# A float32 decoder layer on one core: FFN down products in three parts instead of two, three of eight row pairs by Strassen's seven products

## The chip, the cores and the metric

The kernel runs on one core of one Trainium2 chip. The metric is device time in microseconds (us). Engines are named as in the profile: PE is TensorE (matrix products), PEld its weight loads, DVE VectorE, ACT ScalarE, POOL GpSimd, SP the engine that issues nearly all transfers.

## The reference

One layer on 256 tokens of width 2048, all float32: a half-step FFN, a mixer (attention beside a convolution), a second FFN. Only the FFNs matter here:

```python
def swiglu_ffn(x, w_gate, w_up, w_down):      # 2048 -> 5632 -> 2048
    h = jax.nn.silu(x @ w_gate) * (x @ w_up)
    return h @ w_down

x = layer_norm(ALPHA * x + 0.5 * swiglu_ffn(x, ...), ln1_g, ln1_b)
...
x = layer_norm(ALPHA * x + 0.5 * swiglu_ffn(x, ...), ln3_g, ln3_b)
```

## The kernel before

**Split products.** Each float32 operand is split into `hi` (rounded to the type fp32r) and `lo` = operand - `hi`. A product of a 128x128 block with a 128x512 block is three matmuls into one PSUM bank: hi x hi, hi x lo, lo x hi (`mm3`, lines 465 to 468). "Product" below means these three.

**Weights.** All weights of the layer stream once, as a fixed list `sources` of tiles of 128 x 1024 (two row blocks of 512 columns), in the order of use. `Steps` keeps the stream: SP loads a tile into one of four `raw` buffers, ACT casts it to `hi` (line 133), DVE subtracts to get `lo` (line 135). `hi` and `lo` have a ring of 8 (`RING`); splits run up to 7 tiles ahead of use (`LEAD`). `take` gives PE the next tile, `release` frees its ring place, and `step`, called once per tile, issues two more splits and whatever work was put down for that step with `at`. The order on every engine is that of these calls; each engine's queue is in order.

**FFN.** The 5632 hidden features are 44 blocks of 128, done in two parts of 24 and 20. In a part, the groups come first: for each pair of blocks, `token_group` runs 8 weight tiles (12 matmuls each, 6 for each block of 128 tokens) into two banks, ACT and DVE form silu(gate) * up (`sl`, `ht`, lines 658, 659), DVE transposes it to features (`hf`, line 666, 16 of them, spread over four steps), ACT and DVE split it into `hh` and `hl` (lines 670, 671). Then the down products: `tokens_by` takes the four column chunks of 512 one after the other, each with half as many weight tiles as the part has blocks, 12 matmuls a tile, and adds each finished bank to `xt` (`evacuate`, line 299). The last part's chunks also feed the norm's statistics (line 305). There the second token block lags: the weight tiles of the last 8 steps (6 in the first FFN) are held and used for it at the end, while DVE does the first block's norm (`finish`). In the second FFN that ending holds several finished banks in PSUM (`kept`), and the last tiles' columns are done in two halves (lines 622 to 634).

The sums lie in eight PSUM banks of 512 columns: pools psB and psC with two tiles of one bank, psA with two tiles of two.

## Time and profile before

| | |
|---|---|
| median of 3 runs | 1716.37 us (1715.96 to 1716.41) |
| profiled execution, first to last instruction | 1713.9 us, 2.5 below the median |
| DVE busy | 1183.7 us |
| ACT busy | 808.7 us |
| tiles of w_down | 176 loads of 512 KB |
| transfers | 336.38 MB, mean 196 GB/s |

Of the profiled execution only this span is known, so the 2.5 us are what lies around it, together with the scatter of the runs. "Busy" means that at least one instruction is in flight on the engine: PE's matmuls overlap, so that their durations sum to more than their time. A row such as `L135 DVE ... x45 | 54.8, 1224 | 50.5 <-ACT hi L133` gives a line, engine, operation, operands (out<-in), count, busy us, mean ns of one, and idle us before them with what ended it. A windows row gives, for a stretch of time, each engine's busy us with its count, then the granted PE clock (1.00 is full), the DMA engines' busy share and GB/s. A timeline row starts with start and length in us.

### The profile page before, as it was taken

To read this page: it belongs to the slowest core of one execution; us is meant where nothing else is said; L and a number is where in the kernel's file an instruction comes from. 1 tells how busy PE (TensorE), PEld (TensorE's weight loads), DVE (VectorE), ACT (ScalarE), POOL (GpSimd) and SP (SyncE) were. 2 spreads that over 40 slices of the span, in tenths; PEclk is the share of its full clock that TensorE was granted. 3 is DMA by queue.
4 is the path that set the end of the run, shared out by engine and by line. 5 is a ranking of instruction groups with operands and counts; after the bars stand their busy time and mean duration, and the time that the engine had idled before them with its cause. 6 is when DMAs were issued, how large, how long until landed. Compare 5 with 4: busy or idle time off the path is not lost.

```text
span 1713.9 us, 21604 instructions
## 1 busy us (share of the span) xinstructions
PE 1702.6 (99%) x7857; PEld 1416.3 (83%) x7857; DVE 1183.7 (69%) x2021; ACT 808.7 (47%) x1044; POOL 206.2 (12%) x116
## 2 busy tenths in 40 slices
PE   9999999999999999999999999999999999999997
PEld 7888888888888888888888888888888888888886
DVE  7877776545777765658888788877764467777655
ACT  6544444334444443477665465444443344444431
POOL 0000000000000000168996200000000000000000
PEclk9999999999999999999999999999999999999999
DMA  9766655666656656555754557655556656665662
GB/s 317 259 205 194 195 191 192 196 196 190 193 195 195 191 191 196 170 176 190 203 178 159 196 187 244 209 196 192 192 189 201 194 190 195 196 193 191 233 206 75
DMA packets 96299, 336.38 MB, mean 196 GB/s; under 512 B 11200, under 2 KB 11328, under 8 KB 95936
## 3 DMA queue, kind: packets, MB, share of 16 engines
q1 hardware_dynamic: 96048, 334.74, 60.7%
q8 instruction: 61, 1.00, 0.2%
q14 instruction: 46, 0.38, 0.1%
q10 hardware_dynamic: 144, 0.26, 0.0%
HBM read 332.86 MB, written 2.10 MB: 195 GB/s over the span
## 4 chain that ended last, share of the span: by engine, by line
PE 99%; DVE 0%; DMA 0%; ACT 0%; issue 0%; DVEq 0%; SPq 0%
PE grp L468 18%; PE grp L467 18%; PE grp L466 18%; PE acc L466 11%; PE acc L467 11%; PE acc L468 11%; PE in_c L789 2%; PE in_a L789 2%; PE in_q L789 1%; PE in_a L787 1%; PE in_c L787 1%; PE grp L487 1%; PE grp L488 1%; PE grp L485 1%; PE in_q L787 1%; PE tp L339 0%
## 5 line engine op out<-in xcount | busy, mean ns | idle before, releaser
L133 ACT CAST hi<-raw 128x1024 fp32r<-128x1024 f32 (+1 forms) x616 | 643.0, 1047 | 762.7 <-PE grp L468 357.9
L135 DVE TENSOR_TENSOR lo<-raw,hi 128x1024 fp32r<-128x1024 f32 (+1 forms) x543 | 660.4, 1221 | 386.2 <-ACT hi L133 382.1
L466 PE MATMUL grp<-hi,xcat 128*128 128x512 f32 x1384 | 538.4, 389 | 0.0
L467 PE MATMUL grp<-lo,xcat 128*128 128x512 f32 x1384 | 538.4, 389 | 0.0
L468 PE MATMUL grp<-hi,xcat 128*128 128x512 f32 x1384 | 538.4, 389 | 0.0
L467 PEld LDWEIGHTS grp<-lo,xcat 128*128 128x128 f32 x1384 | 259.8, 188 | 54.1
L466 PEld LDWEIGHTS grp<-hi,xcat 128*128 128x128 f32 x1384 | 259.8, 188 | 53.9
L468 PEld LDWEIGHTS grp<-hi,xcat 128*128 128x128 f32 x1384 | 259.8, 188 | 53.8
L466 PE MATMUL acc<-hi,hh 128*128 128x512 f32 x708 | 274.7, 388 | 0.0
L468 PE MATMUL acc<-hi,hl 128*128 128x512 f32 x708 | 274.6, 388 | 0.0
L467 PE MATMUL acc<-lo,hh 128*128 128x512 f32 x708 | 274.6, 388 | 0.0
L135 POOL TENSOR_TENSOR lo<-raw,hi 128x1024 fp32r<-128x1024 f32 x73 | 175.9, 2432 | 730.3 <-ACT hi L133 723.4
L666 DVE STREAM_TRANSPOSE hf<-ht 32x128 f32<-32x128 f32 x704 | 212.8, 302 | 11.2
L466 PEld LDWEIGHTS acc<-hi,hh 128*128 128x128 f32 x708 | 132.9, 188 | 27.3
L467 PEld LDWEIGHTS acc<-lo,hh 128*128 128x128 f32 x708 | 132.9, 188 | 27.2
L468 PEld LDWEIGHTS acc<-hi,hl 128*128 128x128 f32 x708 | 132.9, 188 | 27.2
L852 DVE SCALAR_TENSOR_TENSOR conv<-hc,cw_sb,conv 128x256 f32<-128x256 f32 x231 | 96.7, 485 | 1.1
L449 POOL TENSOR_SCALAR rs_t<-rs_y,rs_w 128x1 f32<-128x1 f32 x1 | 0.3, 342 | 717.9 <-DVE rs_y L448 717.9
L299 DVE SCALAR_TENSOR_TENSOR xt<-acc,xt 128x512 f32<-128x512 f32 x46 | 31.7, 690 | 54.7 <-PE acc L468 54.7
L658 ACT ACTIVATE sl<-grp 128x256 f32<-128x256 f32 x88 | 33.6, 384 | 56.5 <-PE grp L468 52.7
L466 PE MATMUL acc<-hi,mh 128*128 128x512 f32 x128 | 50.5, 394 | 0.0
L659 DVE TENSOR_TENSOR ht<-sl,grp 128x256 f32<-128x256 f32 x88 | 36.5, 418 | 20.3 <-ACT sl L658 20.2
(149 smaller groups left out, 947.6 us busy)
## 6 DMA issues: line engine op xcount, KB each, us to landing
raw<-in_wu SPq DMA_DIRECT2D x348, 512.0 KB, 4.3
raw<-in_wd SPq DMA_DIRECT2D x176, 512.0 KB, 4.3
raw<-in_win SPq DMA_DIRECT2D x52, 512.0 KB, 4.0
raw<-in_wout SPq DMA_DIRECT2D x32, 512.0 KB, 4.0
xt<-in_xT SPq DMA_DIRECT2D x8, 256.0 KB, 5.8
raw<-in_head SPq DMA_DIRECT2D x8, 256.0 KB, 4.7
xt<-in_x SPq DMA_DIRECT2D x2, 1024.0 KB, 8.0
rg<-in_rows SPq DMA_DIRECT2D x8, 256.0 KB, 4.4
```

What stands on the lines that cost most here:

```text
L133: nc.scalar.copy(hi, raw)
L135: eng.tensor_tensor(out=lo, in0=raw, in1=hi.bitcast(F32), op=ALU.subtract)
L299: nc.vector.scalar_tensor_tensor(out=y, in0=ps, scalar=factor, in1=x_, op0=ALU.mult, op1=ALU.add)
L466: nc.tensor.matmul(ps, s_hi, m_hi, start=start, stop=False)
L467: nc.tensor.matmul(ps, s_hi, m_lo, start=False, stop=False)
L468: nc.tensor.matmul(ps, s_lo, m_hi, start=False, stop=stop)
L658: nc.scalar.activation(sl, ps[b][:, : JG * P], AF.Silu)
L659: nc.vector.tensor_tensor(out=ht[:, b], in0=sl, in1=ps[b][:, JG * P :], op=ALU.mult)
L666: nc.vector.transpose(dst[:, t], src[:, f])
L787: nc.tensor.matmul(ps[:, :S], w[1][:, n], x1[:, k, 0, :], start=False, stop=k == KT - 1)
L789: nc.tensor.matmul(ps, w[0][:, n], x1[:, k], start=k == 0, stop=False)
L852: nc.vector.scalar_tensor_tensor(out=out, in0=x_, scalar=w, in1=acc, op0=ALU.mult, op1=ALU.add)
```

## The change

The hidden blocks are done in three parts (16, 16 and 12). The last is done as before. In the other two, `by_sums` takes two column chunks (a "column pair") at a time and goes through the part's eight pairs of row blocks, each S or C (`CSCSCSCC`). C is as before: two weight tiles, eight products. S is Strassen's scheme in Winograd's form for 2x2 blocks (two row blocks by two column chunks, two token blocks): both tiles of weights are loaded at once (`load_set`), DVE makes four sums of 512 columns from them (`rest`), and 3.5 tiles instead of 2 are split and stand in the ring as four. The hidden side gets four sums of 128 columns and seven blocks instead of four (`group`'s `split`). Seven products go into eight banks (0 to 7; C uses 0, 2, 3, 4, S uses 1 to 7), which collect over all eight row pairs; the output sums are made once per column pair, after the last S (`shared`, five operations and four later adds) and after the last C (four adds to `xt`). Nothing changes in which bytes are loaded. The mixer keeps its order on every engine.

Diff, cut:

```diff
-JA = 24
+PARTS = ((0, 16), (16, 32), (32, 44))
+KINDS = ("CSCSCSCC", "CSCSCSCC", None)
+BLOCKS = {"S": 7, "C": 4}
 JG = 2
 NC_ = D // 512
 HD = 64
...
+            if isinstance(self.sources[n], tuple):
+                if self.opened == 2:
+                    return
+                self.load_set(n)
...
+    def load_set(self, n):
+
+        raws = [self.raw(), self.extra.tile([P, 1024], F32, tag="rawx", name=f"rawx{n}", bufs=2)]
+        self.opened += 1
+        self.loaded += 3
+        for raw, src in zip(raws, self.sources[n][0]):
+            self.nc.sync.dma_start(raw, src)
+        self.jobs += [(n, raws, self.first), (n + 3, raws, self.rest)]
...
+    def upper(self, n, raw):
...
+        pair = [self.pool.tile([P, 1024], F32R, tag=t, name=f"{t}{n}", bufs=RING) for t in ("hi", "lo")]
+        hi, lo = (t[:, : raw.shape[1]] for t in pair)
+        self.nc.scalar.copy(hi, raw)
...
+        def lower():
+            self.nc.vector.tensor_tensor(out=lo, in0=raw, in1=hi.bitcast(F32), op=ALU.subtract)
...
+        return lower
...
+    def first(self, n, raws):
+        raws.append(self.upper(n, raws[0]))
...
+    def rest(self, last, raws):
...
+        n = last - 2
+        a, b = ([r[:, :512], r[:, 512:]] for r in raws[:2])
+        zero = raws[2]
+        sub = self.nc.vector.tensor_tensor
+        self.flush(1)
+        t = self.extra.tile([P, 1024], F32, tag="sum", name=f"sum{n}", bufs=1)
+        sub(out=t[:, :512], in0=b[0], in1=a[0], op=ALU.subtract)
+        sub(out=t[:, 512:], in0=b[1], in1=t[:, :512], op=ALU.subtract)
+        one = self.upper(n, t)
+        sub(out=b[0], in0=b[1], in1=b[0], op=ALU.subtract)
+        two = self.upper(n + 1, raws[1])
+        self.flush()
+        zero()
+        sub(out=a[1], in0=a[1], in1=t[:, 512:], op=ALU.subtract)
+        self.vector(2.4, 0.3)
+        three = self.upper(n + 2, a[1])
+
+        def ended():
+            three()
+            self.open -= 1
+            self.opened -= 1
+            self.load()
+
+        self.pending = [one, two, ended]
...
-        for j0, j1 in ((0, JA), (JA, JT)):
+        for (j0, j1), kinds in zip(PARTS, KINDS):
             for g in range(j0 // JG, j1 // JG):
                 sources.extend(wu[g, q, h] for q in range(4) for h in range(2))
-            for c in range(NC_):
-                sources.extend(wd[c, g, h] for g in range(j0 // 4, j1 // 4) for h in range(2))
+            pairs = [divmod(t, 2) for t in range(j0 // 2, j1 // 2)]
+            if kinds is None:
+                sources.extend(wd[c, g, h] for c in range(NC_) for g, h in pairs)
+                continue
+            for c in range(0, NC_, 2):
+                for kind, (g, h) in zip(kinds, pairs):
+                    both = (wd[c, g, h], wd[c + 1, g, h])
+                    sources.extend(both if kind == "C" else [(both, i) for i in range(4)])
 
     add_ffn(wu1, wd1)
     first = len(sources)
...
+    def by_sums(hh, hl, kinds, factor):
+
+        firsts = [sum(BLOCKS[k] for k in kinds[:t]) for t in range(len(kinds))]
+        final = kinds.rindex("S")
+        for c in range(0, NC_, 2):
+            one, seven = (p.tile([P, 512], F32, tag="acc", name="sum") for p in (psB, psC))
+            mid = psA.tile([P, 2, 512], F32, tag="gu", name="sum")
+            two, four = (p.tile([P, 512], F32, tag="acc", name="sum") for p in (psB, psC))
+            end = psA.tile([P, 2, 512], F32, tag="gu", name="sum")
+            bank = {1: one, 7: seven, 5: mid[:, 0], 6: mid[:, 1], 2: two, 4: four, 3: end[:, 0], 0: end[:, 1]}
+            uses = {k: kinds.count("S") for k in (1, 5, 6, 7)}
+            uses |= {k: kinds.count("S") + 2 * kinds.count("C") for k in (2, 3, 4)} | {0: 2 * kinds.count("C")}
+            left = dict(uses)
+            ys = {(i, j): xt[:, 1 - i, (c + j) * 512 : (c + j + 1) * 512] for i in range(2) for j in range(2)}
+            tmp = {}
+
+            def product(k, block, w, half):
+                cols = slice(half * 512, (half + 1) * 512)
+                left[k] -= 1
+                mm3(
+                    bank[k], hh[:, block], hl[:, block], w[0][:, cols], w[1][:, cols],
+                    left[k] == uses[k] - 1, left[k] == 0,
+                )
+
+            def add(out, k, other):
+                nc.vector.scalar_tensor_tensor(
+                    out=out, in0=bank[k], scalar=factor, in1=other, op0=ALU.mult, op1=ALU.add
+                )
+                st.vector(0.66, 0.3)
+
+            def shared():
+
+                tmp.update((k, act.tile([P, 512], F32, tag="z", name="part", bufs=ZB)) for k in range(4))
+                nc.scalar.mul(tmp[0], bank[1], factor)
+                add(tmp[1], 6, tmp[0])
+                add(tmp[3], 5, tmp[1])
+                add(ys[1, 1], 5, ys[1, 1])
+                add(tmp[2], 7, tmp[1])
+                for n, (at, k) in enumerate((((0, 0), 0), ((0, 1), 3), ((1, 0), 2), ((1, 1), 2))):
+                    st.at(n + 2, lambda y=ys[at], t=tmp[k]: nc.vector.tensor_tensor(
+                        out=y, in0=y, in1=t, op=ALU.add
+                    ), True)
+
+            for t, kind in enumerate(kinds):
+                a = firsts[t]
+                ends = t == len(kinds) - 1
+                if kind == "S":
+                    u = [st.take() for _ in range(2)]
+                    product(1, a, u[0], 0)
+                    product(5, a + 3, u[1], 0)
+                    product(6, a + 4, u[1], 1)
+                    u.append(st.take())
+                    product(7, a + 5, u[2], 0)
+                    st.step(2.7)
+                    product(2, a + 2, u[0], 1)
+                    st.release()
+                    st.release()
+                    product(3, a + 6, u[2], 1)
+                    st.release()
+                    u.append(st.take())
+                    product(4, a + 1, u[3], 0)
+                    st.release()
+                    if t == final:
+                        shared()
+                    st.step(2.0)
+                else:
+                    for i, (p, q) in enumerate(((2, 4), (3, 0))):
+                        w = st.take()
+                        for k, blocks in ((p, (1, 3)), (q, (0, 2))):
+                            for half in range(2):
+                                product(k, a + blocks[half], w, half)
+                        st.release()
+                        if ends:
+                            for k, at in ((p, (0, i)), (q, (1, i))):
+                                add(ys[at], k, ys[at])
+                        st.step()
+                if ends and kind == "S":
+                    for k, at in ((2, (0, 0)), (4, (1, 0)), (3, (0, 1)), (0, (1, 1))):
+                        if uses[k]:
+                            add(ys[at], k, ys[at])
+
     def ffn(xc, tag, skew, begun, prepare, finish, kept=None):
         with tc.tile_pool(name=f"ffn{tag}", bufs=2) as pool:
-            for part, (j0, j1) in enumerate(((0, JA), (JA, JT))):
+            st.extra = pool
+            for part, ((j0, j1), kinds) in enumerate(zip(PARTS, KINDS)):
                 n = j1 - j0
-                hh = pool.tile([P, JA, S], F32R, tag="hh", name=f"hh{part}", bufs=1)
-                hl = pool.tile([P, JA, S], F32R, tag="hl", name=f"hl{part}", bufs=1)
-                def group(j, ps, hh=hh, hl=hl):
-
-                    ht = pool.tile([P, 2, JG * P], F32, tag="ht", name="ht")
-                    hf = pool.tile([P, JG, S], F32, tag="hf", name="hf")
+                ends = part == len(PARTS) - 1
+                blocks = 2 * n if kinds is None else sum(BLOCKS[k] for k in kinds)
+                hh, hl = (pool.tile([P, blocks, P], F32R, tag=t, name=f"{t}{part}", bufs=1) for t in ("hh", "hl"))
+
+                def group(j, ps, hh=hh, hl=hl, kinds=kinds):
+
+                    ht = pool.tile([P, 2, JG * P], F32, tag="ht", name="ht", bufs=1)
+                    hf = pool.tile([P, JG, S], F32, tag="hf", name="hf", bufs=1)
                     for b in range(2):
                         sl = pool.tile([P, JG * P], F32, tag="sl", name="sl")
                         nc.scalar.activation(sl, ps[b][:, : JG * P], AF.Silu)
...
                             dst = hf[32 * f : 32 * f + 32].rearrange("p j (b t n) -> p t b j n", b=2, n=32)
                             nc.vector.transpose(dst[:, t], src[:, f])
 
+                    h4 = hf.rearrange("p j (b n) -> p (j b) n", n=P)
+                    s4 = ht.rearrange("p b (j n) -> p (b j) n", n=P)
+                    t = j // JG
+                    a = 2 * j if kinds is None else sum(BLOCKS[k] for k in kinds[:t])
+
+                    def parted(at, src, eng):
+                        hi, lo = (x_[:, at : at + src.shape[1]] for x_ in (hh, hl))
+                        nc.scalar.copy(hi, src)
+                        eng.tensor_tensor(out=lo, in0=src, in1=hi.bitcast(F32), op=ALU.subtract)
+
                     def split():
-                        js = slice(j, j + JG)
-                        nc.scalar.copy(hh[:, js], hf)
-                        nc.vector.tensor_tensor(out=hl[:, js], in0=hf, in1=hh[:, js].bitcast(F32), op=ALU.subtract)
+                        if kinds is None or kinds[t] == "C":
+                            return parted(a, h4, nc.vector)
+                        for o, x_, y, op in (
+                            (0, h4[:, 0], h4[:, 2], ALU.add), (2, h4[:, 1], h4[:, 0], ALU.subtract),
+                            (1, s4[:, 0], h4[:, 1], ALU.subtract), (3, h4[:, 3], s4[:, 1], ALU.subtract),
+                        ):
+                            nc.vector.tensor_tensor(out=s4[:, o], in0=x_, in1=y, op=op)
+                        parted(a, h4[:, 1:], nc.vector)
+                        parted(a + 3, s4, nc.vector)
 
                     for f in range(4):
                         st.at(1 + f, lambda f=f: turn(f), True)
-                    st.at(5, split, True)
+                    st.at(4, split, True)
 
                 j = 0
                 if xc is xcat and part == 0:
...
-                tokens_by((hh, hl), 0, n, 0.5, stats, (lambda b: finish(b, stats)) if part == 1 else None,
-                          kept if part == 1 else None)
+                if kinds is not None:
+                    by_sums(hh, hl, kinds, 0.5)
+                    continue
+                prepare(pool)
+                stats = new_stats(f"st{tag}", 1 if kept is None else 2)
+                lhs = [x_.rearrange("p (j b) n -> p j (b n)", b=2) for x_ in (hh, hl)]
+                tokens_by(lhs, 0, n, 0.5, stats, lambda b: finish(b, stats), kept)
 
     def params(name):
         return small.tile([P, 2, 4], F32, tag=name, name=name, bufs=1)
```

**Three places in the order**, all on VectorE (DVE). First, the end of the first part's groups. The two `ht` rows are the last group's gate, which waits for the group's last matmuls. Before:

```order
L135 TENSOR_TENSOR lo100_2224<-raw100_2141,hi100_2223 128x1024
L135 TENSOR_TENSOR lo101_2242<-raw101_2163,hi101_2241 128x1024
L135 TENSOR_TENSOR lo102_2260<-raw102_2185,hi102_2259 128x1024
L659 TENSOR_TENSOR ht_2265<-sl_2267,grp0_2101 128x256
L659 TENSOR_TENSOR ht_2265<-sl_2270,grp1_2102 128x256
```

Now (tiles 64, 65 and 70 are plain, 66 to 69 are the first set; `lo64` and `lo65` stand just above):

```order
L167 TENSOR_TENSOR sum67_1560<-rawx66_1422,raw66_1421 128x512
L168 TENSOR_TENSOR sum67_1560<-rawx66_1422,sum67_1560 128x512
L170 TENSOR_TENSOR rawx66_1422<-rawx66_1422 128x512
L143 TENSOR_TENSOR lo66_1516<-raw66_1421,hi66_1515 128x1024
L174 TENSOR_TENSOR raw66_1421<-raw66_1421,sum67_1560 128x512
L143 TENSOR_TENSOR lo67_1564<-sum67_1560,hi67_1563 128x1024
L143 TENSOR_TENSOR lo68_1568<-rawx66_1422,hi68_1567 128x1024
L143 TENSOR_TENSOR lo69_1573<-raw66_1421,hi69_1572 128x512
L207 TENSOR_TENSOR lo70_1589<-raw70_1451,hi70_1588 128x1024
L825 TENSOR_TENSOR ht_1598<-sl_1600,grp0_1433 128x256
L825 TENSOR_TENSOR ht_1598<-sl_1603,grp1_1434 128x256
```

The whole first set has come to stand ahead of the last group's gate.

Second, the change from one column chunk to the next, where banks are read out. Before (`acc0`, `acc1` are the chunk's two banks):

```order
L135 TENSOR_TENSOR lo113_2486<-raw113_2417,hi113_2485 128x1024
L299 SCALAR_TENSOR_TENSOR xt_79<-acc0_2273,xt_79 128x512
L299 SCALAR_TENSOR_TENSOR xt_79<-acc1_2274,xt_79 128x512
L135 TENSOR_TENSOR lo114_2506<-raw114_2435,hi114_2505 128x1024
L135 TENSOR_TENSOR lo115_2526<-raw115_2453,hi115_2525 128x1024
```

Now, from the first column pair to the second (`sum_1609` and `sum_1610` are its banks 2 and 4, `sum_1611` banks 3 and 0):

```order
L753 SCALAR_TENSOR_TENSOR xt_79<-sum_1609,xt_79 128x512
L753 SCALAR_TENSOR_TENSOR xt_79<-sum_1610,xt_79 128x512
L167 TENSOR_TENSOR sum89_1923<-rawx88_1827,raw88_1826 128x512
L168 TENSOR_TENSOR sum89_1923<-rawx88_1827,sum89_1923 128x512
L170 TENSOR_TENSOR rawx88_1827<-rawx88_1827 128x512
L143 TENSOR_TENSOR lo88_1893<-raw88_1826,hi88_1892 128x1024
L174 TENSOR_TENSOR raw88_1826<-raw88_1826,sum89_1923 128x512
L143 TENSOR_TENSOR lo89_1927<-sum89_1923,hi89_1926 128x1024
L767 TENSOR_TENSOR xt_79<-xt_79,part_1859 128x512
L753 SCALAR_TENSOR_TENSOR xt_79<-sum_1611,xt_79 128x512 x2
```

Four sums and two splits of the next set now stand between the reads of banks 2 and 4 and those of banks 3 and 0. The second column pair's banks 5 and 6 are the PSUM place of `sum_1611`: PE's first product into bank 5, the second product of that pair's first set, waits for the last row.

Third, the second FFN's ending, between the first block's norm and the last banks. Before:

```order
L430 SCALAR_TENSOR_TENSOR xt_79<-xt_79,par3_138,b33_13271 128x512
L299 SCALAR_TENSOR_TENSOR xt_79<-acc1_13853,xt_79 128x512
L299 SCALAR_TENSOR_TENSOR acc1_13481<-acc1_13481,xt_79 128x256
L305 BN_STATS st21_13274<-acc1_13481 128x6
L299 SCALAR_TENSOR_TENSOR acc1_13668<-acc1_13668,xt_79 128x256
```

Now:

```order
L512 SCALAR_TENSOR_TENSOR xt_79<-xt_79,par3_138,b33_14027 128x512
L381 SCALAR_TENSOR_TENSOR acc1_14280<-acc1_14280,xt_79 128x512
L387 BN_STATS st21_14030<-acc1_14280 128x6 x2
L381 SCALAR_TENSOR_TENSOR xt_79<-acc1_14366,xt_79 128x512
L381 SCALAR_TENSOR_TENSOR acc1_14165<-acc1_14165,xt_79 128x256
L387 BN_STATS st21_14030<-acc1_14165 128x6
```

Column chunk 2's add for the second token block and its two statistics have moved behind the first block's norm.

More of the change, by code (lines that the diff above doesn't have):

```diff
@@ L74, in __init__ @@
         self.xT, self.x_raw, self.xcat = xT, x_raw, xcat
-        self.loaded = self.open = self.whole = self.done = self.used = self.now = 0
-        self.jobs, self.ready = [], {}
+        self.loaded = self.open = self.opened = self.whole = self.done = self.used = self.now = 0
+        self.jobs, self.ready, self.pending = [], {}, []
         self.later, self.background, self.backlog = [], None, 0.0
@@ L118, in load, with flush @@
             self.jobs.append(("free", None, None))
+    def load_set(self, n):
[11 more added lines that the diff above has]
+            self.nc.vector.tensor_tensor(out=lo, in0=raw, in1=hi.bitcast(F32), op=ALU.subtract)
+            self.vector(1.16, 1.3)
+            self.ready[n] = pair
+            while self.whole in self.ready:
+                self.whole += 1
+        return lower
+    def flush(self, most=9):
+        while most > 0 and self.pending:
+            self.pending.pop(0)()
+            most -= 1
+    def first(self, n, raws):
[23 more added lines that the diff above has]
+        self.pending = [one, two, ended]
     def split(self):
         nc = self.nc
+        if not self.jobs:
+            return self.flush()
         n, raw, at = self.jobs.pop(0)
-        if n is None:
+        if callable(at):
+            at(n, raw)
+            self.load()
+        elif n is None:
             nc.scalar.copy(at[:, :, 0, :], raw)
@@ L133, in split @@
             nc.scalar.copy(hi, raw)
+            self.flush()
             eng = nc.gpsimd if n in self.pooled else nc.vector
@@ L148, in ahead @@
             if n is not None and n >= min(self.used + LEAD, self.done + RING, self.most):
+                self.flush(most)
                 break
@@ L156, in take @@
         while n >= self.whole:
-            self.split()
+            if self.pending:
+                self.flush(1)
+            else:
+                self.split()
         return self.ready.pop(n)
@@ L644, in tokens_by @@
             st.step()
+    def by_sums(hh, hl, kinds, factor):
[57 more added lines that the diff above has]
+                    st.step(2.0)
+                else:
+                    for i, (p, q) in enumerate(((2, 4), (3, 0))):
[12 more added lines that the diff above has]
+                            add(ys[at], k, ys[at])
@@ L687, in ffn @@
                     j += JG
-                if part == 1:
-                    prepare(pool)
-                stats = new_stats(f"st{tag}", 1 if kept is None else 2) if part == 1 else None
-                tokens_by((hh, hl), 0, n, 0.5, stats, (lambda b: finish(b, stats)) if part == 1 else None,
-                          kept if part == 1 else None)
+                if kinds is not None:
+                    by_sums(hh, hl, kinds, 0.5)
+                    continue
+                prepare(pool)
+                stats = new_stats(f"st{tag}", 1 if kept is None else 2)
+                lhs = [x_.rearrange("p (j b) n -> p j (b n)", b=2) for x_ in (hh, hl)]
+                tokens_by(lhs, 0, n, 0.5, stats, lambda b: finish(b, stats), kept)
     def params(name):
@@ L723, in prepare3 @@
         for c in range(NC_):
-            g = pool.tile([P, 512], F32, tag="g3", name=f"g3{c}", bufs=NC_)
+            g = act.tile([P, 512], F32, tag="z", name=f"g3{c}", bufs=ZB)
             nc.sync.dma_start(g, rows[5, c * 512 : (c + 1) * 512].partition_broadcast(P))
```

## The prediction

> **What bounds the kernel now.** I read the page first: busy times, slices, then the chain that ended last.
>
> ```profile
> span 1713.9 us, 21604 instructions
> PE 1702.6 (99%) x7857; PEld 1416.3 (83%) x7857; DVE 1183.7 (69%) x2021; ACT 808.7 (47%) x1044; POOL 206.2 (12%) x116
> PEclk9999999999999999999999999999999999999999
> PE 99%; DVE 0%; DMA 0%; ACT 0%; issue 0%; DVEq 0%; SPq 0%
> ```
>
> The chain is TensorE from end to end. A change gains only what it takes out of TensorE's queue, and loses whatever makes TensorE wait. The windows view shows the two stages in question: gate/up groups (30 to 260), down products (270 to 390 and 1265 to 1385), and ahead of them the start (10 to 30).
>
> ```profile
> core 0: us, PE busy (x) PEld busy (x) DVE busy (x) ACT busy (x) POOL busy (x), PEclk, DMA share, GB/s
> 10.00:30.00 20.00, 20.00 (x90) 16.55 (x89) 15.81 (x18) 13.94 (x18) 0.00 (x0) 1.00 0.98 343
> 30.00:260.00 230.00, 230.00 (x1016) 190.54 (x1015) 174.82 (x298) 109.74 (x124) 1.30 (x3) 1.00 0.66 214
> 270.00:390.00 120.00, 120.00 (x531) 99.40 (x530) 62.06 (x65) 47.11 (x46) 0.00 (x0) 1.00 0.61 194
> 1265.00:1385.00 120.00, 120.00 (x531) 99.36 (x530) 59.08 (x53) 46.41 (x44) 0.00 (x0) 1.00 0.61 193
> ```
>
> TensorE is never idle in either; VectorE is busy 76% of the groups and 52% of the down stage, ScalarE 39% there, GpSimd not at all. So the down stage is where VectorE has room. The price of a matmul is its distance to the next one, not its duration, as the timeline of TensorE shows:
>
> ```profile
> 20.00 0.39 PE L466 MATMUL grp<-hi,xcat 128*128 128x512 f32 x1
> 20.23 0.39 PE L467 MATMUL grp<-lo,xcat 128*128 128x512 f32 x1
> 20.45 0.39 PE L468 MATMUL grp<-hi,xcat 128*128 128x512 f32 x1
> 20.68 0.39 PE L466 MATMUL grp<-hi,xcat 128*128 128x512 f32 x1
> ```
>
> Three matmuls, one product of blocks, start 0.68 us apart: 0.227 each, though each lasts 0.39.
>
> **Removed: one product in eight.** Two parts in each of two FFNs have two column pairs with three Strassen sets each: 24 sets. A set has 7 products where there were 8, so 24 x 3 = 72 matmuls go (the order counts 6963 and 6891 rows on TensorE). Nothing else of TensorE changes in number. 72 x 0.227 = **16.3 us less**. (By duration it would be 28; that would be wrong.)
>
> **Added on VectorE, down stage.** These rows price it:
>
> ```profile
> L135 DVE TENSOR_TENSOR lo<-raw,hi 128x1024 fp32r<-128x1024 f32 x45 | 54.8, 1224 | 50.5 <-ACT hi L133 50.4
> L299 DVE SCALAR_TENSOR_TENSOR xt<-acc,xt 128x512 f32<-128x512 f32 x6 | 4.2, 692 | 7.3 <-PE acc L468 7.3
> L402 DVE TENSOR_TENSOR xt<-xt,rg 128x512 f32<-128x512 f32 x8 | 5.5, 685 | 0.0
> 1002.88 4.63 DVE L135 TENSOR_TENSOR lo<-raw,hi 128x1024 fp32r<-128x1024 f32 x4 [0.26 <-ACT hi L133]
> 1044.15 0.68 DVE L403 TENSOR_TENSOR xt<-xt,rb 128x512 f32<-128x512 f32 x1
> 1044.75 0.69 DVE L671 TENSOR_TENSOR hl<-hf,hh 128x512 fp32r<-128x512 f32 x1
> 715.16 0.69 DVE L299 SCALAR_TENSOR_TENSOR xt<-acc,xt 128x512 f32<-128x512 f32 x1 [5.85 <-PE acc L468]
> 715.88 0.69 DVE L305 BATCH_NORM_STATS2 st<-xt 128x6 f32<-128x512 f32 x1
> ```
>
> A 1024-wide subtraction costs 1.22 alone and (4.63 - 1.22) / 3 = 1.13 in a row; a 512-wide one 0.69, 0.60 in a row, 0.72 if the next reads its result. A set is four 512-wide sums, three 1024-wide splits and one 512-wide: 5 x 0.69 + 3 x 1.22 = 7.1 us by durations, 6.5 in a row, while TensorE spends 7 x 0.68 = 4.8 on it; a plain pair takes 2.4 against 5.4. With the 12 output operations, a column pair asks VectorE for 19 wide and 27 narrow ones: 19 x 1.22 + 27 x 0.69 = 41.8 us by durations, 19 x 1.13 + 27 x 0.60 + 8 x 0.12 = 38.7 in a row. TensorE has 183 x 0.227 = 41.5. That is the risk of this change: VectorE goes from half busy to 93 to 101% of its stage. I take 38.7, since the subtractions do follow each other in a row here, and keep 41.8 as the upper end.
>
> Two things help. VectorE enters ahead: the order puts two plain tiles, a whole set and a third tile (3 x 1.13 + 6.5 = 9.9 us) in front of the last group's gate. Against that stands that group's tail, 2 x 0.42 + 16 x 0.30 + 0.69 = 6.3 us:
>
> ```profile
> L666 DVE STREAM_TRANSPOSE hf<-ht 32x128 f32<-32x128 f32 x704 | 212.8, 302 | 11.2
> 265.91 0.42 DVE L659 TENSOR_TENSOR ht<-sl,grp 128x256 f32<-128x256 f32 x1
> ```
>
> Two column pairs are then 2 x 38.7 + 6.3 - 9.9 = 73.8 us of VectorE (80.0 by durations) under 83 us of TensorE. TensorE waits for no split: cost 0.
>
> **The tightest place** is the bank pair that the second column pair takes over. TensorE reaches it 2.72 + 5.44 + 0.68 = 8.8 us after the last product into bank 4 ended. From there VectorE's queue has one output add, four sums, two wide splits, a 512-wide add and two output adds: 0.61 + 0.72 + 3 x 0.60 + 2 x 1.13 + 0.60 + 0.61 + 0.69 = 7.3 us (8.0 by durations). It starts late by the signal, which a silu row gives: its last matmul started at 264.57, the silu at 265.06.
>
> ```profile
> 264.57 0.39 PE L468 MATMUL grp<-hi,xcat 128*128 128x512 f32 x1
> 265.06 0.39 ACT L658 ACTIVATE sl<-grp 128x256 f32<-128x256 f32 x1 [0.32 <-PE grp L468]
> ```
>
> So 0.49 from that start, 0.26 from the product's end: 8.8 - 0.3 = 8.5 available against 7.3 to 8.0. Margin 0.5 to 1.2 us, four times in the program. Cost 0; without the margin every us over costs 4.
>
> **Added in the groups.** Three groups in eight make four 128-wide sums and split seven blocks, not four. No such sum is in the trace; the 256-wide row (0.42) bounds it above, nothing below: 0 to 1.7 us, and a half more split (0.5). VectorE goes from 16.5 to at most 18.7 of a group's 21.8 us. ScalarE gains casts of 1.05 us and stays under 60%. Hidden; they would cost only if VectorE's lead of seven tiles were gone.
>
> **Moved: transfers.** The bytes stay. A set loads two tiles at once, 1.05 MB in 4.8 us, 220 GB/s, where the start of the kernel ran at 343.
>
> ```profile
> raw<-in_wd SPq DMA_DIRECT2D x176, 512.0 KB, 4.3
> ACT hi L133 <- DMA raw<-in_wd: 5.2, 1, 5.2
> ```
>
> The one load queued behind a set's release is the last plain tile of a column pair; landing 4.3 us later it holds ScalarE's casts and VectorE's output adds some 2 us, and then VectorE would have waited for bank 2 anyway: by the starts above it gets there after 6.3 + 38.7 - 9.9 - 3.6 (six output operations still to come) + 2.3 (two tiles of the next pair) + 1.5 (waits for the silu and a cast) = 35.3 us of the pair, and TensorE closes bank 2 at 41.5 - 5.44 + 1.36 = 37.4. Cost 0, between 0 and 2 us for each of 8.
>
> **The tail gets longer.** The last part now has six tiles a column, and eight are held back for the second token block: two belong to column 2. Its output add and two statistics move behind the first block's norm, whose last operations are the 2.74 us row:
>
> ```profile
> 1699.16 2.74 DVE L430 SCALAR_TENSOR_TENSOR xt<-xt,par,b 128x512 f32<-128x512 f32 x4
> 1701.82 0.69 DVE L299 SCALAR_TENSOR_TENSOR xt<-acc,xt 128x512 f32<-128x512 f32 x1
> 1702.62 0.43 DVE L299 SCALAR_TENSOR_TENSOR acc<-acc,xt 128x256 f32<-128x256 f32 x1
> 1703.09 0.43 DVE L305 BATCH_NORM_STATS2 st<-acc 128x6 f32<-128x256 f32 x1
> 1704.06 0.43 DVE L299 SCALAR_TENSOR_TENSOR acc<-acc,xt 128x256 f32<-128x256 f32 x1 [0.54 <-PE acc L468]
> 1704.99 0.37 DVE L414 BATCH_NORM_AGGREGATE par<-st 128x2 f32<-128x48 f32 x1
> ```
>
> They take 0.72 + 2 x 0.43 = 1.6 us. VectorE had gaps of 0.11 (before 1702.62) and 0.54 (before 1704.06), and some 0.1 is won by running without waits. 1.6 - 0.7 = **0.8 to 1.0 more**; I take 0.8.
>
> **Sum.** -16.3 + 0.8 = -15.5. On the profiled span 1713.9 - 15.5 = 1698.4; the median of the runs, 1716.4, stands 2.5 above that span, so **1700.9 us**.
>
> **The rivals.** (a) *The handover or the casts slip* by 0.5 to 2 us at the eight column pairs: VectorE by durations leaves 0.5 us of margin, and its in-order queue puts a late cast in front of the bank reads. 1704.9 at 0.5 a pair, 1708.9 at 1. For it: 93% busy; against: the lead of 10 us and the margins above. (b) *No change*: transfers of a set land late. 15.5 / 24 = 0.65 us a set eats all: 1716. Against: 343 GB/s, and one wait for such a load in the whole trace. (c) *Slower, VectorE is the bound.* It decides when a column pair needs over 41.5 + 15.5 / 8 = 43.4 us, 12% above 38.7. The trace has a 512-wide split that is that slow:
>
> ```profile
> L1021 DVE TENSOR_TENSOR ml<-sw,mh 128x512 fp32r<-128x512 f32 x4 | 4.1, 1066 | 2.3 <-ACT mh L1020 2.3
> ```
>
> At 1.07 us the 27 narrow operations add 27 x 0.38 = 10.3: 52 a pair, 10.6 over, 8 x 10.6 = 85: 1786. Against: its output is scattered, the sums here are contiguous like L402's. (d) *TensorE's clock drops* because each product now goes to another bank. At half clock in the sets alone 24 x 21 x 0.227 = 114 us more: 1815. Against: the rows at 20.00 to 20.68 change bank every three matmuls at 0.227, clock 1.00. The Trainium skill (TensorE: Matmul & The Clock Gate, A second HAM failure mode: psum-queue depth-cycling) has a kernel that cycled through PSUM banks idle often enough for the clock to swing; by that rule (d) happens, and the trace does not agree with it.
>
> The Trainium skill (VectorE: DVE Perf Modes, The DRAIN you can't avoid) holds that the next operation starts only when the pipe is empty. By that rule a pair would cost 41.8, not 38.7, and the margin at the bank would be the smaller one; the row of four at 1002.88 starts every 1.13 for 1.22 lasting, so here the measurement decides.
>
> **Chances.** Forecast 0.72, (a) 0.14, (b) 0.05, (c) 0.06, (d) 0.03. The low end is 1699.5 (no tail cost, and 0.6 of spread); the high end 1708 takes in (a) nearly whole; (b) to (d) and the rest of (a) are left out. Faster by over 0.2% (3.4 us, about what a measurement here tells from no change) is forecast and (a): 0.86; same 0.05; slower 0.09.
>
> **What would show it.** Right: 7785 matmuls on TensorE, no idle at the products after the first plain pair of a second column pair, down stage at 0.227, VectorE near 1184 + 24 x 4.7 (a set less two plain tiles) + 80 x 0.69 (12 output operations in each of 8 column pairs, less 16 that go) + 12 x 1.7 = 1372 us, the last aggregation 0.8 later after TensorE's end. Wrong: TensorE waiting for `lo` or an output add in the sets, a granted clock under 1, sums above 0.69 us.

## The result and the profile after

The changed kernel takes **1701.42 us**, median of 4 runs (1701.29 to 1702.42); the kernel before, run beside it, 1716.21 (1715.96 to 1716.41). The ratio is 0.9915, interval 0.9901 to 0.9929: 14.8 us faster, against 15.5 forecast and a predicted time of 1700.9.

The page of the changed kernel, the lines that answer to those shown of before:

```profile
span 1700.6 us, 21870 instructions
PE 1687.1 (99%) x7785; PEld 1402.5 (82%) x7785; DVE 1344.6 (79%) x2305; ACT 847.6 (50%) x1112; POOL 206.3 (12%) x116
PEclk9999999999999999999999999999999999999999
PE 98%; DVE 1%; DMA 0%; issue 0%; ACT 0%; SPq 0%; DVEq 0%
```

7785 matmuls, 72 fewer; the chain is still TensorE, the clock full. VectorE is at 79% of the span, from 69%. The windows view shows the down stage of the first part (180 to 263) and that of the second FFN's second part (1410 to 1493):

```profile
180.40:263.20 82.80, 82.80 (x367) 68.54 (x367) 75.55 (x99) 41.98 (x46) 0.00 (x0) 1.00 0.58 190
1409.90:1492.80 82.90, 82.90 (x367) 68.68 (x366) 75.48 (x99) 42.55 (x47) 0.00 (x0) 1.00 0.57 190
```

TensorE is never idle there, though VectorE went from about half busy to 91% (75.55 of 82.80, 75.48 of 82.90). The waits of TensorE, complete down to 0.2 us, hold no row with `sum`, the name of every product in the new loop:

```profile
PE grp L642 <- ACT hi L204: 1.6, 2, 1.1
PE idle L327 <- DVE ones L324: 1.2, 1, 1.2
PE acc L548 <- DVE st L387: 0.8, 1, 0.8
```

The first row is the start of this one execution: TensorE waited 1.15 us at 7.60 us for the first weights. The profiled run was the slowest of the four (1702.42); the spans of the other three are 1699.5 to 1699.7. The time of a run stands 1.8 above its span (1702.42 against 1700.6), so 0.7 of the prediction's 2.5 was scatter; the times, 1701.4 against 1700.9, are the better comparison. The third row is the tail, below.

The tightest place: VectorE's timeline where the first column pair hands its bank pair to the second, from the output add of bank 2 on (start, duration; in brackets the wait and its releaser):

```profile
218.05 0.69 DVE L753 SCALAR_TENSOR_TENSOR xt<-sum,xt 128x512 f32<-128x512 f32 x1 [0.41 <-PE sum L550]
219.41 0.69 DVE L753 SCALAR_TENSOR_TENSOR xt<-sum,xt 128x512 f32<-128x512 f32 x1 [0.67 <-PE sum L550]
220.02 0.68 DVE L167 TENSOR_TENSOR sum<-rawx,raw 128x512 f32<-128x512 f32 x1
220.74 0.69 DVE L168 TENSOR_TENSOR sum<-rawx,sum 128x512 f32<-128x512 f32 x1
221.35 0.69 DVE L170 TENSOR_TENSOR rawx<-rawx 128x512 f32<-128x512 f32 x1
221.95 1.22 DVE L143 TENSOR_TENSOR lo<-raw,hi 128x1024 fp32r<-128x1024 f32 x1
223.20 0.69 DVE L174 TENSOR_TENSOR raw<-raw,sum 128x512 f32<-128x512 f32 x1
223.81 1.22 DVE L143 TENSOR_TENSOR lo<-sum,hi 128x1024 fp32r<-128x1024 f32 x1
224.95 0.69 DVE L767 TENSOR_TENSOR xt<-xt,part 128x512 f32<-128x512 f32 x1
225.55 1.28 DVE L753 SCALAR_TENSOR_TENSOR xt<-sum,xt 128x512 f32<-128x512 f32 x2
```

The order is the one the prediction worked through, and from bank 4's add (219.41) to the end of the last one (226.83) it took 7.4 us; predicted were 7.3. The two waits in brackets, 0.41 and 0.67 us, are the time that VectorE has to spare close ahead of the handover. They are the reserve that several experiments below use up.

### The profile page after: what moved, and what is told of

Same layout as the page of the kernel before. It is cut to its first block, busy times and chain, and to the rows that moved or that the text cites. A ratio compares the mean times of both kernels' runs of the same rounds, so it can differ in the third digit from the quotient of the medians.

```text
span 1700.6 us, 21870 instructions
## 1 busy us (share of the span) xinstructions
PE 1687.1 (99%) x7785; PEld 1402.5 (82%) x7785; DVE 1344.6 (79%) x2305; ACT 847.6 (50%) x1112; POOL 206.3 (12%) x116
## 4 chain that ended last, share of the span: by engine, by line
PE 98%; DVE 1%; DMA 0%; issue 0%; ACT 0%; SPq 0%; DVEq 0%
PE grp L549 18%; PE grp L550 18%; PE grp L548 18%; PE sum L548 7%; PE sum L550 6%; PE sum L549 6%; PE acc L548 4%; PE acc L550 4%; PE acc L549 4%; PE in_c L973 2%; PE in_a L973 2%; PE in_q L973 1%; PE in_a L971 1%; PE in_c L971 1%; PE grp L569 1%; PE grp L570 1%
## 5 line engine op out<-in xcount | busy, mean ns | idle before, releaser
L207 DVE TENSOR_TENSOR lo<-raw,hi 128x1024 fp32r<-128x1024 f32 (+1 forms) x495 | 596.6, 1219 | 208.9 <-ACT hi L204 204.1
L548 PE MATMUL sum<-hi,hh 128*128 128x512 f32 x488 | 189.9, 389 | 0.0
L549 PE MATMUL sum<-lo,hh 128*128 128x512 f32 x488 | 189.9, 389 | 0.0
L550 PE MATMUL sum<-hi,hl 128*128 128x512 f32 x488 | 189.9, 389 | 0.0
L550 PEld LDWEIGHTS sum<-hi,hl 128*128 128x128 f32 x488 | 91.6, 188 | 19.2
L549 PEld LDWEIGHTS sum<-lo,hh 128*128 128x128 f32 x488 | 91.6, 188 | 18.9
L548 PEld LDWEIGHTS sum<-hi,hh 128*128 128x128 f32 x488 | 91.6, 188 | 18.9
L548 PE MATMUL acc<-hi,hh 128*128 128x512 f32 (+1 forms) x196 | 75.8, 387 | 0.9 <-DVE st L387 0.8
L550 PE MATMUL acc<-hi,hl 128*128 128x512 f32 (+1 forms) x196 | 75.6, 385 | 0.0
L549 PE MATMUL acc<-lo,hh 128*128 128x512 f32 (+1 forms) x196 | 75.4, 385 | 0.0
```

Source lines behind the costliest of these rows:

```text
L207: eng.tensor_tensor(out=lo, in0=raw, in1=hi.bitcast(F32), op=ALU.subtract)
L548: nc.tensor.matmul(ps, s_hi, m_hi, start=start, stop=False)
L549: nc.tensor.matmul(ps, s_hi, m_lo, start=False, stop=False)
L550: nc.tensor.matmul(ps, s_lo, m_hi, start=False, stop=stop)
```

## The experiments

Each time stands beside a run of the kernel before on the same chip (medians 1715.96 to 1716.33), over five rounds.

**Arrangement alone.** All products plain, three parts kept:

```diff
-KINDS = ("CSCSCSCC", "CSCSCSCC", None)
+KINDS = ("CCCCCCCC", "CCCCCCCC", None)
-        final = kinds.rindex("S")
+        final = kinds.rfind("S")
```

> Three parts and column pairs as in the change, but every row pair plain: no Strassen set at all. If the gain is the 72 matmuls alone, all of it goes, and what the new arrangement costs shows: about 1.0 for the longer ending and 0.6 for TensorE's wait for the last group's hidden blocks, so 1717.2 to 1718.5. If the arrangement in three parts brings part of the gain, the time lies below 1714.

1718.19 us (1717.65 to 1718.51), ratio 1.0011 [1.0003, 1.002]. The arrangement by itself costs 1.9 us, so the gain is wholly the matmuls'.

**Two and four sets** in place of three: `CSCCSCCC` and `CSCSCSSC` in the same line.

> Two sets in a column pair instead of three: 8 sets fewer, 24 matmuls more. If VectorE is covered everywhere and only TensorE's count acts, 8 x 0.68 = 5.4 more than the change: 1706.8. If VectorE already costs time in the sets (its queue 93 to 101% full), less is lost than 5.4, or nothing: 1701 to 1705.

1706.79 us (1706.52 to 1707.18), ratio 0.9945 [0.9933, 0.9958]. From two to three sets a column pair (8 sets in all) the time falls by 5.4 us, 0.67 a set: three matmuls of 0.227, nothing lost.

> Four sets in a column pair (CSCSCSSC): TensorE alone would need 5.4 less than the change: 1696.0. A column pair then asks VectorE for 42.9 us, started one behind the other, under 40.8 of TensorE; two pairs eat some 5.5 us of the 7 to 10 us of lead. Theory of the covered VectorE: the lead lasts, 1696 to 1699. Theory that VectorE's share of the stage decides: it is the bound from here on, 1701 or more, with TensorE idle in the second column pairs.

1706.41 us (1706.3 to 1707.39), ratio 0.9944 [0.9931, 0.9956], where 1696 was to be had. Of the two cases that I had set down, full cover was the wrong one: the fourth set loses 10 us. TensorE and its weight loads now wait at the handover (four times) and for `lo`:

```profile
PE sum L548 <- DVE xt L753: 5.9, 4, 1.7
PE sum L549 <- DVE lo L143: 1.3, 4, 0.3
...
PEld sum L548 <- ACT hi L204: 7.4, 4, 2.1
PEld sum L549 <- DVE lo L143: 4.5, 8, 0.8
```

The first row of each engine is the same four stalls. The matmul's row names the output add that it waits for; the weight load ahead of it is put down to a cast, which is no more than the last signal the profile saw there. By the starts of the matmuls the four handovers lose 6.5 us and the sets behind them 4.0: the whole loss.

**Four sets with less VectorE work.** ScalarE waited 2.9 us for a late load in that run, so the loads were suspect too. This kernel has the four sets but leaves out two of a set's four block sums, so its output isn't the layer's:

```diff
-        sub(out=b[0], in0=b[1], in1=b[0], op=ALU.subtract)
...
-        sub(out=a[1], in0=a[1], in1=t[:, 512:], op=ALU.subtract)
```

> Four sets in each column pair, as in the kernel that ran at 1706.4 us, but two of the four block sums of a set (those for products two and three) are left out, so the output is not the reference's; loads, casts, splits and matmuls are those of the four sets. VectorE's column pair falls from 43.5 to 43.5 - 4 x 2 x 0.60 = 38.7 us. If VectorE's work is what took the gain from the four sets: TensorE is covered again, 1701.4 - 8 x 0.68 = 1696.0, between 1695.5 and 1697.5 us. If the late load (ScalarE waited 2.9 us for a plain tile) and the casts behind it are what holds: still 1703 to 1706.5 us.

1696.63 us (1695.89 to 1697.76), ratio 0.9887 [0.9873, 0.99], and no `sum` product waits. Loads, casts and matmuls are those of the four sets. It was VectorE's work that took the gain, not the transfers: ScalarE's waits for tiles of w_down (`hi` on `raw<-in_wd`) fell with it, from 9.6 us to 3.4 in all.

**Share or handover?** Two kernels add VectorE work without changing a result. One repeats each output add of a column pair into a spare buffer, so that the work falls into the handover:

```diff
                             for k, at in ((p, (0, i)), (q, (1, i))):
+                                add(spare, k, ys[at])
                                 add(ys[at], k, ys[at])
```

> Each of the four output additions at the end of a column pair is done once more into a spare buffer (the result is not changed). That adds 4 x 0.61 = 2.4 us of VectorE to a column pair of 38.7 us, which stays below TensorE's 41.5 us, but it puts three of the four into the chain that frees the bank pair: 7.4 + 3 x 0.61 = 9.2 us against the 8.5 us that TensorE leaves. If the handover is the tightest place: a stall of 0.5 to 0.9 us at each of four places, 1703.3 to 1705.0 us, and a wait of a sum product for the output addition in the trace at the four places. If only the share of VectorE over a column pair counts: no change, 1701.0 to 1701.8 us.

1706.61 us (1706.02 to 1706.93), ratio 0.9944 [0.9931, 0.9956]: 5.2 us slower than the changed kernel, though VectorE's column pair, 38.7 + 4 x 0.72 = 41.6 us, only comes level with TensorE's 41.5. I had expected 1703.3 to 1705.0, with 0.61 an add. What waits is the product that takes over the bank, for the four adds at the end of the handover:

```profile
PE sum L548 <- DVE xt L754: 3.7, 4, 0.9
```

That is its row in the waits view. In the timeline:

```profile
225.99 0.68 DVE L754 SCALAR_TENSOR_TENSOR spare<-sum,xt 128x512 f32<-128x512 f32 x1
226.71 0.69 DVE L754 SCALAR_TENSOR_TENSOR xt<-sum,xt 128x512 f32<-128x512 f32 x1
227.31 0.68 DVE L754 SCALAR_TENSOR_TENSOR spare<-sum,xt 128x512 f32<-128x512 f32 x1
228.03 0.69 DVE L754 SCALAR_TENSOR_TENSOR xt<-sum,xt 128x512 f32<-128x512 f32 x1
...
227.54 0.39 PE L550 MATMUL sum<-hi,hl 128*128 128x512 f32 x1
228.87 0.47 PE L548 MATMUL sum<-hi,hh 128*128 128x512 f32 x1 [0.94 <-DVE xt L754]
```

An extra add delays the next operation by 0.72 us here (225.99 to 226.71). Three of them lie in the chain: 2.16 us. TensorE's product starts 1.33 after the one before it, in place of 0.227: 1.10 lost. So the margin of the changed kernel was 2.16 - 1.10 = **1.06 us**, within the 0.5 to 1.2 of the prediction. The changed kernel's own trace says the same: there the product that takes over the bank starts at 228.05, VectorE is done at 226.83, and from the end of the last add to the waiting product are 0.15 us (228.72 to 228.87 above), which leaves 1.07. The waits view has four stalls of nearly the same length. Four times 1.10 make 4.4 of the 5.2; the first matmul after each takes 0.30 to the next (228.87 to 229.17), 0.3 more in all; about half a microsecond isn't placed.

The other kernel makes the first block sum of a set several times, work that is spread over the sets:

```diff
         sub(out=t[:, :512], in0=b[0], in1=a[0], op=ALU.subtract)
+        sub(out=t[:, :512], in0=b[0], in1=a[0], op=ALU.subtract)
+        sub(out=t[:, :512], in0=b[0], in1=a[0], op=ALU.subtract)
```

> The first block sum of every set is made three times in place of once (the same values again). 3 sets x 2 x 0.60 = 3.6 us more VectorE work in a column pair, 42.3 us against TensorE's 41.5. If the share over a whole part counts, with the head start of 9.9 us and the tail of 6.3: 2 x 42.3 + 6.3 - 9.9 = 81.0 us under 83, no change, 1701.0 to 1701.8. If the average of one column pair counted: (42.3 - 41.5) x 8 = 6.4 us slower, 1707.8. If the handover decides: 7.4 + 1.2 = 8.6 us against 8.5, 0 to 1 us slower, at most 1702.5.

1714.2 us (1712.86 to 1716.65), ratio 0.9988 [0.9979, 0.9997]: 12.8 us lost, more than in any of the three cases that I had set down (none, up to one, 6.4). The head start of 9.9 us that my working counted on does not reach this place. The wait behind VectorE's first set, ahead of the last group; the wait for the column pair's last plain tile; the two output adds at the handover; and TensorE's product:

```profile
178.66 1.23 DVE L209 TENSOR_TENSOR lo<-raw,hi 128x1024 fp32r<-128x1024 f32 x1 [0.32 <-ACT hi L206]
...
213.05 1.22 DVE L209 TENSOR_TENSOR lo<-raw,hi 128x1024 fp32r<-128x1024 f32 x1 [1.33 <-ACT hi L206]
...
220.19 1.28 DVE L755 SCALAR_TENSOR_TENSOR xt<-sum,xt 128x512 f32<-128x512 f32 x2
...
229.79 0.47 PE L550 MATMUL sum<-hi,hh 128*128 128x512 f32 x1 [1.95 <-DVE xt L755]
```

The same places in the changed kernel:

```profile
179.06 1.23 DVE L207 TENSOR_TENSOR lo<-raw,hi 128x1024 fp32r<-128x1024 f32 x1 [1.77 <-ACT hi L204]
210.42 1.23 DVE L207 TENSOR_TENSOR lo<-raw,hi 128x1024 fp32r<-128x1024 f32 x1 [1.20 <-ACT hi L204]
```

A set's two repeats cost 2 x 0.72 = 1.44 us. The first set's went into a wait (1.77 became 0.32). The two sets behind the last group's gate have nothing of that kind: the wait at 210.42 for the column pair's last plain tile is not slack, for it stayed (1.33) while the whole row moved 2.6 us later: that load goes out when VectorE has finished with the set ahead of it (issued at 205.84 in the changed kernel and 208.35 here, each within 0.04 us of the end of that set's last split). So 2.88 us meet the 0.41 + 0.67 in front of bank 2 and bank 4, and VectorE is 1.8 late there; the next set's repeats add 1.44 in the chain, and the margin takes back 1.06: 2.2 lost. The trace has 229.79 - 227.45 - 0.23 = 2.1 (the matmul before started at 227.45). The waits view has four of these, and weight loads that wait for `lo`. The windows row shows what came behind the third of them:

```profile
PE sum L550 <- DVE xt L755: 7.5, 4, 2.0
...
PEld sum L551 <- DVE lo L143: 2.8, 6, 0.6
1208.60:1212.00 3.40, 3.40 (x10) 2.62 (x9) 3.40 (x5) 0.00 (x0) 0.00 (x0) 0.50 0.45 141
```

By the starts of the matmuls the four handovers lose 8.1 of the 12.8 us. The waits for `lo` lose about 2: a weight load's wait runs beside matmuls, so its 2.8 is not all lost. And for 3.4 us the granted clock was 0.50, with matmuls 0.43 apart, which makes 1.6. The whole would also fit a plain mean over a column pair, (38.7 + 6 x 0.72 - 41.5) x 8 = 12; but that mean gives 0.8 for the longer handover, against 5.2, and (42.9 - 40.8) x 8 = 17 for the four sets, against 10.4.

> The same sum made seven times: 3 x 6 x 0.60 = 10.8 us more in a column pair, 49.5 us. If VectorE's share over a part becomes the bound: 2 x 49.5 + 6.3 - 9.9 = 95.4 against 82.8 us, 12.6 us in each of four parts, 1740 to 1755 us. If only the handover counts: 7.4 + 3.6 = 11.0 against 8.5 us, 2.5 us four times, about 1711.5. If VectorE work in the sets is never the limit: 1701.

1778.78 us (1776.21 to 1782.99), ratio 1.0366 [1.0352, 1.038]. VectorE is the bound now:

```profile
PE sum L555 <- DVE lo L143: 37.3, 30, 4.4
PE sum L554 <- DVE xt L759: 12.1, 4, 3.0
```

The waits are in the splits of the sets more than at the handover. By 0.72 a repeat a column pair needs 38.7 + 18 x 0.72 = 51.7, (51.7 - 41.5) x 8 = 81; measured 77. My 1740 to 1755 was too low, by the price (0.60) and by the head start, which was counted whole in every part.

**The table load.** The change exposes a wait in the second FFN's last part that I hadn't predicted. All engines of the changed kernel there:

```profile
1624.06 1.28 ACT L906 ACT_TABLE_LOAD   x1
...
1626.53 1.23 DVE L207 TENSOR_TENSOR lo<-raw,hi 128x1024 fp32r<-128x1024 f32 x1 [2.03 <-ACT hi L204]
...
1636.57 0.62 ACT L841 CAST hh<-hf 128x512 fp32r<-128x512 f32 x1 [3.71 <-DVE hf L832]
...
1636.77 0.39 PE L550 MATMUL acc<-hi,hl 128*128 128x512 f32 x1
1637.24 0.19 PEld L548 LDWEIGHTS acc<-hi,hh 128*128 128x128 f32 x1 [0.51 <-ACT hh L841]
...
1637.97 0.19 PEld L550 LDWEIGHTS acc<-hi,hl 128*128 128x128 f32 x1 [0.43 <-DVE hl L842]
...
1638.78 0.40 PE L550 MATMUL acc<-hi,hl 128*128 128x512 f32 x1
```

ScalarE loads the square root's table in front of its casts; VectorE's split waits 2.03 us, the last group's transposes behind it end late, and TensorE waits for `hh`, then `hl`: from 1636.77 to 1638.78 are six matmuls, 2.01 us where their pace makes 1.36, so 0.65 is lost. With 6 tiles a column the last group's blocks are needed at the 6th tile, before at the 10th. The experiment puts the square root eight steps later:

```diff
-        nc.scalar.activation(small.tile([P, 1], F32, tag="rs_v", name="rs_s"), eps, AF.Sqrt)
+        st.at(8, lambda: nc.scalar.activation(small.tile([P, 1], F32, tag="rs_v", name="rs_s"), eps, AF.Sqrt))
```

> The change, with ScalarE's square root that is put ahead of the last down stage (and its table load, 1.28 us) moved eight steps later. If that load is why TensorE waits for the last group's hidden blocks, the 0.6 us go: 1700.8, no wait of TensorE's weight loads for hh or hl in the second FFN. If the part's six tiles are too short a cover by themselves, the wait stays: 1701.4.

1701.05 us (1700.64 to 1702.24), ratio 0.9913 [0.9899, 0.9926]. The weight loads' two waits for `hh` and `hl` are gone from the waits view, so the cause is shown; 0.4 us less than the changed kernel is less than the two intervals can tell apart. It is the lowest median here of a kernel that computes the whole layer.

**Sums on GpSimd.** If VectorE's work is what limits four sets, GpSimd could take some, being idle in the down stage. One kernel gives it a set's fourth sum, the next the third as well; both have the later table load:

```diff
-        sub(out=a[1], in0=a[1], in1=t[:, 512:], op=ALU.subtract)
+        self.nc.gpsimd.tensor_tensor(out=a[1], in0=a[1], in1=t[:, 512:], op=ALU.subtract)
```

> Four sets in each column pair, the fourth block sum of every set made by GpSimd in place of VectorE (a GpSimd addition of this size takes 1.30 us in the trace, VectorE's 0.69), and the square root's table load put later. VectorE's column pair falls from 43.5 to 43.5 - 4 x 0.60 = 41.1 us, and one sum leaves the chain of the handover. What the four sets lost at each handover was 10.4 / 4 = 2.6 us, of which 2.4 + 0.6 = 3.0 us now go: if VectorE's work ahead of the handover is the limit, 1696.0 to 1697.5 us, no wait of a sum product over 0.3 us. If GpSimd holds VectorE up or its 1.3 us stand in the chain of casts, the sum products wait for lo: 1699 to 1706 us.

> The same with the third and the fourth block sum of every set on GpSimd: VectorE as in the run that left both sums out, which took 1696.6 us. If VectorE's work is the limit and GpSimd's is free: 1695.5 to 1697.0 us (the later table load is in it). If the two sums on GpSimd, 2 x 1.30 = 2.6 us one behind the other in place of 2 x 0.60, hold the casts and so VectorE's splits: 1698 to 1706 us, with ScalarE waiting for rawx and raw of GpSimd.

1715.82 us (1715.25 to 1718.04), ratio 1.0 [0.9991, 1.0009], and 1730.23 us (1729.81 to 1730.73), ratio 1.0083 [1.0069, 1.0097]. Each sum given away made it slower, by 9 and 14 us, outside every range that I had set down. The timeline of VectorE and GpSimd in a set of the first:

```profile
189.37 1.22 DVE L143 TENSOR_TENSOR lo<-sum,hi 128x1024 fp32r<-128x1024 f32 x1
189.53 2.20 POOL L174 TENSOR_TENSOR raw<-raw,sum 128x512 f32<-128x512 f32 x1 [13.49 <-DVE lo L143]
190.50 2.31 DVE L143 TENSOR_TENSOR lo<-rawx,hi 128x1024 fp32r<-128x1024 f32 x1
```

GpSimd's sum lasts 2.20 us (mean 2.17 of 32) where its additions of that size took 1.32 elsewhere in the same trace, and VectorE's split beside it 2.31 in place of 1.22. The times fit work that alternates, which is read from them and was not tested by itself: GpSimd ends 1.14 us after VectorE's first split did (190.59 to 191.73), VectorE's next ends 1.08 after GpSimd (192.81). The move takes 0.60 us from VectorE and costs it 1.09.

Not all of the 9 us is that price. The handover's wait is twice that of the four sets (5.9), and behind it the granted clock is 0.50 for some microseconds:

```profile
PE sum L548 <- DVE xt L753: 12.0, 4, 3.2
1210.70:1216.80 6.10, 6.10 (x14) 4.76 (x15) 6.10 (x8) 1.61 (x2) 0.00 (x0) 0.50 0.53 162
```

Matmuls start 0.427 apart there. This follows all four handovers. By the starts of the matmuls the handovers lose 12.6 us in this trace and the slow stretches 8.7; in the four sets, where the clock stayed at 1.00, the handovers lose 6.5.

## Why the prediction was right, step by step

**Removed matmuls.** Right. 0.67 a set from two to three sets, against 3 x 0.227 = 0.68.

**VectorE in the sets.** The durations were right: the sums 0.69, the wide splits 1.22 in the rows above. They follow each other at 0.60 (220.74, 221.35, 221.95), so the lower price, 38.7 a pair, was the one to take; here each starts 0.07 to 0.09 us before the one ahead has ended. The Trainium skill (VectorE: DVE Perf Modes, The DRAIN you can't avoid) says that the next operation waits for an empty pipe, but adds that one that is not held (its word) starts earlier; the prediction cited only the first half, and these rows agree with the second. Busy time came to 1344.6 where I forecast 1372: I had added durations, which count the overlapping ends twice. With 6.5 - 2 x 1.13 = 4.24 a set and 0.61 an output add it is 1183.7 + 24 x 4.24 + 80 x 0.61 + 12 x 1.7 = 1355. The other 10 us aren't placed: the groups' added sums and splits measure 12.8 and 6.9 us, about the 20.4 counted for them.

**Cover.** The verdict was right, "TensorE waits for no split: cost 0", but one line of its reason wasn't. "73.8 us of VectorE under 83 us of TensorE" reads like 9 us in reserve a part. There are 1.08 us close ahead of the handover (the two waits) and 1.06 in it (the longer handover), and the repeated sums agree with both: 2.2 us of loss worked out, 2.1 found. The head start ends in a wait ahead of the last group, and the late load travels with VectorE. My 35.3 against 37.4 us at bank 2 was nearer, 2.1 us; the trace of after shows 0.41 at that bank, and 0.67 more at bank 4.

**The handover.** Right, place and size: 7.4 us against 7.3, margin 1.06 against "0.5 to 1.2 us, four times in the program".

**Transfers.** Right. The last plain tile's load holds VectorE 1.20 us at 210.42, and VectorE still waits for bank 2 behind it; TensorE for nothing.

**The tail.** Mis-sized: 0.8 was taken, 1.0 came. Last operations of the changed kernel on VectorE, and TensorE beside it:

```profile
1684.82 2.74 DVE L512 SCALAR_TENSOR_TENSOR xt<-xt,par,b 128x512 f32<-128x512 f32 x4
1687.48 0.69 DVE L381 SCALAR_TENSOR_TENSOR acc<-acc,xt 128x512 f32<-128x512 f32 x1
1688.20 0.76 DVE L387 BATCH_NORM_STATS2 st<-acc 128x6 f32<-128x256 f32 x2
...
1690.76 0.43 DVE L381 SCALAR_TENSOR_TENSOR acc<-acc,xt 128x256 f32<-128x256 f32 x1 [0.20 <-PE acc L550]
1691.23 0.43 DVE L387 BATCH_NORM_STATS2 st<-acc 128x6 f32<-128x256 f32 x1
1691.69 0.37 DVE L496 BATCH_NORM_AGGREGATE par<-st 128x2 f32<-128x48 f32 x1
...
1689.02 0.39 PE L548 MATMUL acc<-hi,hh 128*128 128x256 f32 x1 [0.78 <-DVE st L387]
```

From the 2.74 us row to the aggregation are 6.87 us, before 1704.99 - 1699.16 = 5.83: 1.04 more. Column 2's add and statistics (1687.48, 1688.20) stand there as forecast. What I left out is that TensorE's last product waits 0.78 us for these statistics, and so VectorE again 0.20 for that product. This is read from the trace; no run moved it.

**Not foreseen.** The table load, 0.65 us. The prediction went through VectorE's lead and ScalarE's share of busy time in the groups, not through what ScalarE does once ahead of the last group.

**The account.** -16.3 + 1.04 + 0.65 = -14.6; measured -14.8. The all-plain kernel has the two costs without the gain: +1.7 against a measured +1.9.

**The rivals.** (a) did not come, and the margin of 1.06 says how near it was. (b) fell: four sets load more tiles in twos and, with less VectorE work, run at 1696.6. (c) is real, and its point of decision was about right: forecast was a pair of 43.4 us for losing the whole gain; at 43.0, the sums made three times, 12.8 of the 14.8 us were gone. That is luck in part: two thirds of that loss sat at the handovers, which (c) did not go by. (d) fell: products that go to another bank each ran at 0.227 with a granted clock of 0.998. The Trainium skill's case (TensorE: Matmul & The Clock Gate, A second HAM failure mode: psum-queue depth-cycling) has TensorE idle between groups of matmuls; the changed kernel's down stages have no such idle time. Where the experiments made TensorE wait long enough, the clock did halve, as the rows at 1208.60 and 1210.70 show.

## What to carry to other kernels

Trading matrix work for vector work pays only up to the place where the vector engine's in-order queue has to hand something back by a date, here a PSUM bank; work out the reserve there, not over the stage. A wait on a transfer counts as reserve only if the transfer isn't itself released by the engine that waits. Moving element work to GpSimd is not free for VectorE: measure the pair together. A stall of TensorE can cost more than its own length; look at the granted clock behind it.

## What the runs showed of the hardware

GpSimd and VectorE, each reading two operands from SBUF, slowed each other down: 2.17 us for a sum that takes GpSimd 1.32 elsewhere in the same kernel, 2.31 for a split that takes VectorE 1.22, the ends lying as if they ran in turns. The Trainium skill (SBUF — State Buffer, Who interferes with whom) says that a VectorE instruction with two SBUF inputs contends with a GpSimd instruction that reads SBUF, and that the shared port pair is an exclusive lock; the rows agree. The favourable cases of my expectations had GpSimd's work free; the others allowed for a delay, but for less than came.

In the rows above, a VectorE operation of 512 columns started 0.72 us after the one ahead where it read or overwrote that one's result, or overwrote what that one read (the add to `xt` behind its repeat into `spare`, 225.99 and 226.71), and 0.60 otherwise. Reading the same PSUM bank was not enough for the 0.72: in the changed kernel two adds that both read bank 5, one into `part` and one into `xt`, started 0.61 apart (212.28 and 212.89).

The granted clock was 0.50 for 3 to 7 us behind all eight handover stalls of 3.0 to 3.5 us in the two GpSimd kernels, behind one of four of 2.0 to 2.1 us (the sums made three times), and behind none of those of 1.1 us (longer handover) and 1.4 to 1.8 us (four sets). The sums made seven times, with stalls up to 4.6 us, show such stretches too.
